# Log-softmax backward on one core: stores moved to a second DMA queue, one group at a time

## Chip, cores, metric

One core of one Trainium2 chip. The metric is device time in microseconds (us) of one execution; each time below is the median of several.

## The reference

```python
def reference(y, dy):                  # both 8 x 1024 x 8192, float32
    softmax_x = np.exp(y)
    sum_dy = np.sum(dy, axis=-1, keepdims=True)
    return dy - softmax_x * sum_dy
```

8192 rows of 8192 elements: 268 MB each of y, dy and output, 805 MB in all, with a few operations per element.

## The kernel before

A group is 256 rows, two per partition, so one partition's share of a tensor is one contiguous run of 64 KiB in HBM. There are 32 groups, two dy tiles `x0` and `x1` (64 KiB per partition each; the result overwrites dy in place) and one y tile of the same size. The parts that matter:

```python
    def sums(x):                       # row 0 on VectorE, row 1 on ScalarE
        ...
        nc.vector.tensor_reduce(out=s_t[:, 0:1], in_=x[:, :D], ..., negate=True)
        for h in range(2):
            nc.scalar.activation(copied[:], x[:, D + h * H : D + (h + 1) * H],
                                 COPY, accum_out=half_t[:, h : h + 1])
        ...
    def compute(x, s_t, r):            # three pieces of a row
        for b, e in PIECES:
            cs = slice(r * D + b, r * D + e)
            nc.scalar.activation(y_t[:, cs], y_t[:, cs], EXP)
            nc.vector.scalar_tensor_tensor(out=x[:, cs], in0=y_t[:, cs], ...)

    for g in range(0, G, 2):           # every DMA on SyncE's queue
        load_dy(g, x_ts[0])
        load_y(g, 0, W)
        s_t = sums(x_ts[0])
        for r in range(R):
            compute(x_ts[0], s_t, r)
        load_dy(g + 1, x_ts[1])
        s_t = sums(x_ts[1])
        for r in range(R):
            load_y(g + 1, r * D, (r + 1) * D)
            compute(x_ts[1], s_t, r)
        for j in range(2):             # a batch of two stores
            nc.sync.dma_start(out=out_v[g + j], in_=x_ts[j][:])
```

So four loads of 8.4 MB (the last in two halves) are followed by two stores of 8.4 MB, all in one queue.

## Time and profile before

| | |
|---|---|
| time, median of 3 | 1867.44 us (1866.99 to 1867.85) |
| moved | 805.3 MB, 432 GB/s over the span |
| busy | DMA 99.9%, VectorE 46%, ScalarE 37% |

The page's rate in 40 equal slices of the span (bytes counted where a packet starts, so single slices jitter by a few per cent):

```profile
GB/s 427 424 430 427 430 447 427 427 431 445 427 427 441 426 437 434 438 431 427 437 438 429 433 428 440 434 431 437 425 438 436 433 436 425 439 433 436 434 428 391
```

**A measure used throughout.** A packet is one contiguous run that one of the 16 DMA engines moves. The trace records each packet's start, duration, size and queue. In an undisturbed stretch a 64 KiB packet takes 2.418 us and one of 32 KiB 1.213 us (in the whole trace before, where all 32 KiB packets are y loads, their median is 1.214). Everything above that, summed over all packets and divided by 16, I call *packet excess*; the time, averaged over the engines, in which an engine had no packet between the first and the last packet is *idle*. With the undisturbed time of all packets the three add up to the span to within 1 us where packets have 32 and 64 KiB: neighbouring packets of one engine overlap by 3 to 4 ns in the records, and this makes up for the 3 us before the first and after the last packet.

### The profile page before, as it was taken

The numbers are of one execution on the slowest core, as the hardware profiler recorded it, in microseconds if no ns is written. First come the engines' busy times: TensorE is split into PE (matmuls) and PEld (weight loads), VectorE is DVE, ScalarE is ACT, GpSimd is POOL, SyncE is SP. The second block draws the span as 40 slices with busy tenths as digits, with TensorE's granted clock in tenths as the row PEclk, the third lists the DMA queues.
The fourth block names the chain that finished last, engine by engine and source line by source line (L and its number), as shares of the span: only waits on it lengthen the run. The fifth ranks groups of instructions, "written<-read, shape, count | busy, mean of one in ns | idle before, by whom it ended". The sixth has DMA issues, their size and how long they took to land.

```text
span 1865.9 us, 923 instructions
## 1 busy us (share of the span) xinstructions
DVE 859.8 (46%) x256; ACT 698.7 (37%) x321; POOL 0.2 (0%) x4
## 2 busy tenths in 40 slices
DVE  2907429074290732807328073280632806338063
ACT  2606326063260532605336052360523605236052
POOL 0000000000000000000000000000000000000000
DMA  9999999999999999999999999999999999999999
GB/s 427 424 430 427 430 447 427 427 431 445 427 427 441 426 437 434 438 431 427 437 438 429 433 428 440 434 431 437 425 438 436 433 436 425 439 433 436 434 428 391
DMA packets 16135, 805.37 MB, mean 432 GB/s; under 512 B 1792, under 2 KB 1792, under 8 KB 1792
## 3 DMA queue, kind: packets, MB, share of 16 engines
q1 hardware_dynamic: 16128, 805.31, 99.9%
q14 instruction: 7, 0.06, 0.0%
HBM read 536.87 MB, written 268.44 MB: 432 GB/s over the span
## 4 chain that ended last, share of the span: by engine, by line
DMA 64%; DVE 13%; ACT 10%; another core or an unknown queue 9%; issue 1%; SPq 0%; DVEq 0%; ACTq 0%
DMA x<-in_dy_dram 31%; DMA out_dram<-x 30%; DVE x L81 13%; ACT copied L61 6%; ACT y_t L80 4%; DMA y_t<-in_y_dram 3%; SPq L75 0%; DVEq L128 0%; ACTq L128 0%; SPq L52 0%; ACTq L80 0%; ACTq L61 0%
## 5 line engine op out<-in xcount | busy, mean ns | idle before, releaser
L81 DVE SCALAR_TENSOR_TENSOR x<-y_t,s_t,x 128x3072 f32<-128x3072 f32 (+1 forms) x192 | 579.4, 3059 | 255.7 <-ACT y_t L80 255.7
L57 DVE TENSOR_REDUCE s_t<-x 128x1 f32<-128x8192 f32 x32 | 277.8, 8682 | 722.3 <-DMA x<-in_dy_dram 722.3
L80 ACT ACTIVATE y_t<-y_t 128x3072 f32<-128x3072 f32 (+1 forms) x192 | 460.1, 2466 | 269.4 <-DMA y_t<-in_y_dram 253.2
L61 ACT ACTIVATE copied<-x 128x4096 f32<-128x4096 f32 x64 | 229.6, 3587 | 864.9 <-DMA x<-in_dy_dram 863.9
L61 ACT ACTIVATION_READ_ACCUMULATOR copied<-x 128x1 f32 x64 | 11.9, 186 | 0.0
L64 DVE TENSOR_SCALAR s_t<-half_t 128x1 f32<-128x1 f32 x32 | 6.5, 204 | 0.0
L61 ACT ACT_TABLE_LOAD x1 | 1.3, 1283 | 0.7 <-PEq L117 0.7
L117 POOL MEMSET const-bfloat16-1.0<- 128x1 bf16 x1 | 0.1, 101 | 0.0
L117 POOL MEMSET const-uint8-127<- 128x1 uint8 x1 | 0.1, 101 | 0.0
L117 POOL MEMSET const-float32-0.0<- 128x1 f32 x1 | 0.1, 98 | 0.2 <-issue 0.2
L117 POOL MEMSET const-float32-1.0<- 128x1 f32 x1 | 0.1, 98 | 0.0
## 6 DMA issues: line engine op xcount, KB each, us to landing
y_t<-in_y_dram SPq DMA_DIRECT2D x32, 4096.0 KB, 18.1
x<-in_dy_dram SPq DMA_DIRECT2D x32, 48.3
out_dram<-x SPq DMA_DIRECT2D x32, 32.5
y_t<-in_y_dram SPq DMA_DIRECT2D x16, 57.6
```

The costliest lines, as they stand in the source:

```text
L57: nc.vector.tensor_reduce(out=s_t[:, 0:1], in_=x[:, :D], axis=mybir.AxisListType.X, op=ALU.add, negate=True)
L61: nc.scalar.activation(copied[:], x[:, D + h * H : D + (h + 1) * H], COPY, accum_out=half_t[:, h : h + 1])
L64: nc.vector.tensor_scalar(out=s_t[:, 1:2], in0=half_t[:, 0:1], scalar1=half_t[:, 1:2], scalar2=-1.0, op0=ALU.add, op1=ALU.mult,)
L80: nc.scalar.activation(y_t[:, cs], y_t[:, cs], EXP)
L81: nc.vector.scalar_tensor_tensor(out=x[:, cs], in0=y_t[:, cs], scalar=s_t[:, r : r + 1], in1=x[:, cs], op0=ALU.mult, op1=ALU.add,)
L117: nc = _bacc.Bacc("TRN2", target_bir_lowering=False, num_devices=1)
```

## The change

Its intent: let each group's store go as soon as the group is ready, on a queue of its own, so that loads never stand behind stores; load y by halves; drop the batches of two. The sum of the second row becomes one ScalarE instruction. The core of the diff (the first part replaces the two 4096-wide copies into PSUM by one of 8192 in place, and makes `load_y` take a row number):

```diff
...
-        for h in range(2):
-            nc.scalar.activation(
-                copied[:], x[:, D + h * H : D + (h + 1) * H], COPY, accum_out=half_t[:, h : h + 1]
-            )
+        nc.scalar.activation(x[:, D:], x[:, D:], COPY, accum_out=second_t[:])
...
-    for g in range(0, G, 2):
-        load_dy(g, x_ts[0])
-        load_y(g, 0, W)
-        s_t = sums(x_ts[0])
+    for g in range(G):
+        x = x_ts[g % 2]
+        load_dy(g, x)
+        s_t = sums(x)
         for r in range(R):
-            compute(x_ts[0], s_t, r)
-        load_dy(g + 1, x_ts[1])
-        s_t = sums(x_ts[1])
-        for r in range(R):
-            load_y(g + 1, r * D, (r + 1) * D)
-            compute(x_ts[1], s_t, r)
-        for j in range(2):
-            nc.sync.dma_start(out=out_v[g + j], in_=x_ts[j][:])
+            load_y(g, r)
+            compute(x, s_t, r)
+            if g == G - 1:
+                if r == 0:
+                    nc.sync.dma_start(out=out_v[g - 1], in_=x_ts[(g - 1) % 2][:])
+                nc.sync.dma_start(out=out_v[g][:, r * D : (r + 1) * D], in_=x[:, r * D : (r + 1) * D])
+        if g < G - 2:
+            nc.scalar.dma_start(out=out_v[g], in_=x[:])
 
 
 # ---- launch: one core; inputs and outputs as the reference has them ----
```

More of the change, by code (lines that the diff above doesn't have):

```diff
@@ L35 @@
     assert N == G * P * R and D == 8192 and G % 2 == 0
-    H = D // 2
     PIECES = [(0, 2048), (2048, 5120), (5120, D)]
@@ L45 @@
     stats = ctx.enter_context(tc.tile_pool(name="stats", bufs=3))
-    psum = ctx.enter_context(tc.tile_pool(name="psum", bufs=1, space=bass.MemoryType.PSUM))
     x_ts = [pool.tile([P, W], fp32, name=f"x{j}") for j in range(2)]
     y_t = pool.tile([P, W], fp32, name="y_t")
-    copied = psum.tile([P, H], fp32, name="copied")
     def load_dy(g, x):
@@ L55, in sums @@
         s_t = stats.tile([P, R], fp32, name="s_t")
-        half_t = stats.tile([P, 2], fp32, name="half_t")
+        second_t = stats.tile([P, 1], fp32, name="second_t")
         nc.vector.tensor_reduce(
@@ L59, in sums, with load_y @@
         )
-        for h in range(2):
-            nc.scalar.activation(
-                copied[:], x[:, D + h * H : D + (h + 1) * H], COPY, accum_out=half_t[:, h : h + 1]
-            )
+        nc.scalar.activation(x[:, D:], x[:, D:], COPY, accum_out=second_t[:])
         nc.vector.tensor_scalar(
-            out=s_t[:, 1:2],
-            in0=half_t[:, 0:1],
-            scalar1=half_t[:, 1:2],
-            scalar2=-1.0,
-            op0=ALU.add,
-            op1=ALU.mult,
-        )
-        return s_t
-    def load_y(g, lo, hi):
-        nc.sync.dma_start(out=y_t[:, lo:hi], in_=y_v[g][:, lo:hi])
+            out=s_t[:, 1:2], in0=second_t[:], scalar1=-1.0, scalar2=None, op0=ALU.mult
+        )
+        return s_t
+    def load_y(g, r):
+        nc.sync.dma_start(out=y_t[:, r * D : (r + 1) * D], in_=y_v[g][:, r * D : (r + 1) * D])
     def compute(x, s_t, r):
```

## The prediction

> **What bounds the kernel now.** I read the page first, for which resource is full; then the DMA windows, for whether reads and writes go at different rates; then the SyncE queue's waits; then the timeline of the last 60 us.
>
> From the page:
>
> ```profile
> span 1865.9 us, 923 instructions
> DVE 859.8 (46%) x256; ACT 698.7 (37%) x321; POOL 0.2 (0%) x4
> DMA  9999999999999999999999999999999999999999
> q1 hardware_dynamic: 16128, 805.31, 99.9%
> HBM read 536.87 MB, written 268.44 MB: 432 GB/s over the span
> ```
>
> VectorE and ScalarE are busy less than half of the time; the DMA engines are at 90% or more in all 40 slices, and the packets of the one hardware queue fill 99.9% of 16 engines' span. The kernel is a copy with arithmetic hidden in it: 805.3 MB that the change does not reduce.
>
> From the windows, one inside a phase of stores and one inside a phase of loads (columns: window, length, busy time of the engines, clock, DMA share, GB/s):
>
> ```profile
> 84.00:118.00 34.00, 8.80 (x3) 4.97 (x2) 0.00 (x0) 1.00 1.00 432
> 124.00:176.00 52.00, 23.38 (x7) 21.74 (x10) 0.00 (x0) 1.00 1.02 444
> ```
>
> Bytes are counted where a packet starts, so short windows jitter by a few per cent. The packet records beneath them are sharper: a packet is one contiguous run in one partition; the 10,240 packets of 64 KiB have a median of 2.418 us and the 4,096 of 32 KiB one of 1.213 us, for loads and stores alike. 65,536 B in 2.418 us is 27.1 GB/s, times 16 engines 433.7 GB/s. Both directions run at the engines' own rate.
>
> From the waits of SyncE's queue:
>
> ```profile
> SPq L75 <- DMA y_t<-in_y_dram: 614.4, 16, 40.0
> SPq L102 <- DVE x L81: 466.3, 16, 29.9
> SPq L52 <- DMA out_dram<-x: 385.1, 30, 18.8
> ```
>
> The queue waits a lot, but the engines have work queued during each of these waits, so none reaches the end of the kernel. Because everything is in one queue in program order, loads and stores hardly ever mix: about 78 us of loads, then 39 us of stores, 16 times.
>
> From the timeline, the end:
>
> ```profile
> 1826.53 7.22 ACT L80 ACTIVATE y_t<-y_t 128x2048 f32<-128x2048 f32 x3 [2.49 <-DMA y_t<-in_y_dram]
> 1834.46 3.41 DVE L81 SCALAR_TENSOR_TENSOR x<-y_t,s_t,x 128x3072 f32<-128x3072 f32 x1
> 1837.90 0.34 SPq L102 DMA_DIRECT2D out_dram<-x  x1
> ```
>
> The last half of y lands at 1826.5 and its arithmetic ends at 1837.9, 11.4 us later. Meanwhile the last-but-one store, 8.4 MB, keeps the DMA engines busy, and the final store follows without a hole. This tail is hidden now.
>
> **What the Trainium skill says.** "DMA: Bandwidth & Descriptors", section "Where 436 GB/s comes from", gives 16 ports of 32 bytes at 850 MHz, 435.2 GB/s. The trace agrees: 432 over the span, 433.7 inside a packet. So 805.3 MB need at least 1850 us, and no order of transfers can gain 2%. The same page, "Issuing engines are not separate DMA queues", says that queues of several issuing engines share the same 16 DMA engines and interleave, and that a second issuer saves only issue time; the kernel before has one queue, so its trace cannot show it. Its section "Queues, rings and completion order" adds that an engine alternates between queues by packet; I use that below to say who finishes when. "ScalarE: Activation LUTs", section "What ACT_TABLE_LOAD costs", gives 186 ns + 0.833 ns per element for an ACTIVATE with immediate operands: 3.60 us for 4096 elements, and the trace has 3.587.
>
> **The change part by part.**
>
> *Sum on ScalarE.* 64 copies of 128x4096 into PSUM (3.587 us each, plus 0.186 to read the accumulator) become 32 in place of 128x8192. By the skill's line these take 7.01 us, so 32 x (2 x 3.77 - 7.20) = 11 us less ScalarE time in the whole kernel. All of it is beside a full DMA: worth 0.
>
> *y in halves.* 16 loads of 8.4 MB become 32 of 4.2 MB; counted per engine, y goes from 128 + 256 packets (64 and 32 KiB) to 512 of 32 KiB. One 64 KiB packet is 2.418, two of 32 KiB are 2.426: 128 x 0.008 = +1.0 us. The final store in halves adds a few hundredths.
>
> *Stores at once, on ScalarE's queue.* Does the DMA keep work? I follow one steady group in packets of one engine (8 per transfer). Take time 0 as store g issuing, right after the last arithmetic on group g. In SyncE's ring there are then the last 3 of 8 packets of dy(g+1), 8 of y's first half, and y's second half becomes issuable at this moment (its buffer is free). Alternating: 3 x (2.42 + 2.42) = 14.5 us; then the store's other 5 packets against 5 of y: 5 x (2.42 + 1.21) = 18.2. Store g lands at about 33 us, and only then may dy(g+2) start, into the same buffer. But SyncE's ring still holds 3 + 8 packets of y, 13.3 us, while a new issue needs 0.4 us and the first packet comes some 1.0 us after the issue (0.73 to 1.75 us at the start of this trace). So no hole. y's second half lands at 46 us, its arithmetic takes the 11.4 us from above, and during it 5 packets of dy(g+2) run: 12 us. Store g+1 then issues at 58 us, with 3 packets of dy left: the cycle closes, at 25.17 MB / 0.4325 = 58.2 us per group, which is the DMA's time. Sums (8.7 us VectorE) fall before y needs them. ScalarE now waits in its own instruction stream for VectorE before each store, about 3 us per group with at least 20 us idle: 0.
>
> *The tail.* "Last two stores behind all loads" is not what the instruction order shows. SyncE's final sequence is: dy(31), y(31) first half, store 30, first half of store 31 (which waits for the arithmetic on that half), y(31) second half, second half of store 31. So the last 4.2 MB load is the last thing in the ring, behind 12.6 MB of stores. When it lands, nothing is left to move until its arithmetic is done: some 0.7 us to landing and release, 11.4 of arithmetic, 0.3 issue, 1.0 to the first packet: a hole of 13.4 us, where the kernel before has none.
>
> Sum without any price of mixing: 1867.4 + 1.0 + 13.4 - 0.5 (a few fixed pauses at the 15 phase changes that go) = 1881 us.
>
> **The rivals.**
>
> 1. *Mixing costs.* After the change each engine switches between a load and a store packet about 8 times in each of 30 groups, 240 turns, where the kernel before has 16 in each direction. For: in its packet records the last y packets before each change to stores are longer than 1.213 us, by 0.006 to 0.2 us per engine, median 0.11 (the very first change 1.0); that is the only place where packets are regularly slow. If each turn cost this, 240 x 0.11 = 26 us, 1907 us. Also, someone wrote batches of two on one queue into a tuned kernel, presumably for a reason. Against: store-to-load changes show no excess; and late in the kernel, where the engines have drifted apart by about 2.5 us and some load while others store, the packets keep 2.418 us. I give a price of some size 40%, and 12 to 15 us as its mean.
>
> 2. *A starved DMA.* Stores share the ring time with loads, so store g lands after 33 us instead of 19, and dy(g+2) waits for it. If round-robin favoured loads more than I assume, the ring could run dry. Against: 13 us of slack above. A hole of 2 us per group would make 1940. I give this 8%.
>
> 3. *More overlap.* Two queues could hide the 8 ns that each packet now pays over its 2.409 us at the skill's rate, and the pauses. At best 1850 + 16.5 = 1867: the same as before. "Perfetto Trace Analysis", section "DMA Optimizations", recommends separate issuers for input and output where it allows more spread; here the spread has nothing to fill. 12%.
>
> 4. *The tail is hidden after all*, if the hardware starts the last load earlier than the queue's order. Against: the order of waits in one queue is fixed. 5%; 1868.
>
> **Range and chances.** 1881 us is the plain sum; 40% of a mixing price of 12 to 15 us gives 1886. Low end: rivals 3 or 4, 1868. High end: a full mixing price and some hole, 1925. Slower by over 2% begins at 1904.8, which needs at least 24 us beyond the tail's 13.4; I give that 0.22. Faster by over 2% is excluded by the 1850 us floor.
>
> **What would show it.** Right: DMA slices of 9 to the last but one, a last slice with a clear dip; a timeline that ends with a y load landing, 11.4 us of arithmetic and then a 4.2 MB store alone; packets of 64 KiB still at 2.42 us; the store's time to landing near 33 us; ScalarE's queue waiting on VectorE. Mixing right: packets of 64 KiB longer while both queues are active, GB/s in all middle slices below 425. Starving right: 8s in the DMA line and compute waiting longer for dy. Wrong altogether: a time under 1870, with no hole before the last store, or over 1925.

## More of the kernel before

For the kernel before: 1858.0 + 4.6 + 2.9 = 1865.5 us, against a span of 1865.9. The three terms are worked out from the packet records; the profile's page does not print them.

## The result, and the profile after

| | before | after |
|---|---|---|
| time, median (range), 4 runs each | 1867.64 us (1866.99 to 1868.19) | 1931.18 us (1923.86 to 1938.28) |
| ratio | 1 | 1.034 (95%: 1.030 to 1.038) |
| packets undisturbed + excess + idle | 1858.0 + 4.6 + 2.9 | 1859.1 + 52.5 + 17.7 |

The change costs 63.5 us, 3.4%. In terms of the ledger: +1.1 from shorter packets, **+47.9 from packets that take longer**, +14.8 from engines with nothing to do.

The page after:

```profile
span 1929.3 us, 933 instructions
...
DVE 862.2 (45%) x256; ACT 691.1 (36%) x257; POOL 0.2 (0%) x4
...
DMA  9999999999999999999999999999999999999996
GB/s 413 424 435 435 446 435 432 422 435 427 403 424 421 418 426 430 427 406 414 421 425 409 408 421 419 421 423 405 420 418 418 420 402 421 427 419 415 422 425 271
...
q1 hardware_dynamic: 14256, 553.65, 67.6%
q10 hardware_dynamic: 4320, 251.66, 31.5%
...
HBM read 536.87 MB, written 268.44 MB: 417 GB/s over the span
```

HBM now moves 417 GB/s over the span in place of 432. Two things are to be seen. The last slice is down to 6 and 271 GB/s: a hole at the end. And the rate sags: the first ten slices are as before, and from the eleventh on most are between 403 and 427, while the DMA line still reads 9. The engines are busy all the time and move less. "Busy" does not tell the two apart; only the rate does.

The stretches make the sag plainer (columns: window, length, busy time of VectorE, ScalarE and GpSimd, clock, DMA share, GB/s). The kernel before:

```profile
500.00:800.00 300.00, 152.41 (x46) 123.36 (x56) 0.00 (x0) 1.00 1.00 432
...
1400.00:1700.00 300.00, 142.35 (x41) 116.34 (x54) 0.00 (x0) 1.00 1.00 432
```

The changed kernel:

```profile
100.00:280.00 180.00, 86.05 (x27) 69.42 (x27) 0.00 (x0) 1.00 1.01 437
500.00:800.00 300.00, 134.71 (x40) 107.78 (x40) 0.00 (x0) 1.00 1.00 423
...
1400.00:1700.00 300.00, 134.71 (x40) 107.78 (x40) 0.00 (x0) 1.00 1.00 417
```

In its first 280 us the changed kernel runs at full rate although its two queues already alternate; the sag comes later. It comes from some of the packets: from 500 to 1700 us the median 64 KiB packet still takes 2.418 us, but 27% of those on ScalarE's queue take over 0.1 us more, and their mean is 2.564 us.

The timeline shows the same in the distance between stores. These are four of the 30 issues on ScalarE's queue (start, length, engine, line, operation), two early neighbours and two late ones:

```profile
112.46 0.36 ACTq L93 DMA_DIRECT2D out_dram<-x  x1
...
170.51 0.36 ACTq L93 DMA_DIRECT2D out_dram<-x  x1
...
1728.56 0.36 ACTq L93 DMA_DIRECT2D out_dram<-x  x1
...
1788.65 0.36 ACTq L93 DMA_DIRECT2D out_dram<-x  x1
```

Early, a group takes 58.05 us, the 58.2 of the prediction's cycle; late, 60.09 us. The next dy load waits until the store from its tile has landed; from the waits of SyncE's queue (total, times, longest) and the page's list of DMA issues (the last number is the median time from issue to landing):

```profile
SPq L51 <- DMA out_dram<-x: 1121.7, 30, 39.3
...
out_dram<-x ACTq DMA_DIRECT2D x30, 38.9
```

The end, from the timeline:

```profile
1879.15 0.55 SPq L66 DMA_DIRECT2D y_t<-in_y_dram  x1
...
1906.04 7.22 ACT L71 ACTIVATE y_t<-y_t 128x2048 f32<-128x2048 f32 x3 [31.47 <-DMA y_t<-in_y_dram]
...
1910.63 6.75 DVE L72 SCALAR_TENSOR_TENSOR x<-y_t,s_t,x 128x3072 f32<-128x3072 f32 x2 [0.30 <-ACT y_t L71]
1917.41 0.33 SPq L91 DMA_DIRECT2D out_dram<-x  x1
```

The last half of y lands at 1906.0, its store issues at 1917.4, and in between there is nothing to move. Where the timeline of before had a store of 8.4 MB beside this arithmetic, there is now none.

### The profile page after: what moved, and what is told of

Read it like the earlier page. It is cut to its first block, busy times and chain, and to the rows that moved or that the text cites. A ratio compares the mean times of both kernels' runs of the same rounds, so it can differ in the third digit from the quotient of the medians.

```text
span 1929.3 us, 933 instructions
## 1 busy us (share of the span) xinstructions
DVE 862.2 (45%) x256; ACT 691.1 (36%) x257; POOL 0.2 (0%) x4
## 4 chain that ended last, share of the span: by engine, by line
DMA 80%; DVE 11%; ACT 8%; issue 0%; DVEq 0%; ACTq 0%; SPq 0%
DMA y_t<-in_y_dram 80%; DVE x L72 11%; ACT y_t L71 8%; DVEq L119 0%; ACTq L119 0%; ACTq L71 0%; SPq L51 0%; SPq L91 0%; SPq L66 0%
## 5 line engine op out<-in xcount | busy, mean ns | idle before, releaser
L59 ACT ACTIVATE x<-x 128x8192 f32<-128x8192 f32 x32 | 225.0, 7030 | 557.8 <-DMA x<-in_dy_dram 557.8
L59 ACT ACTIVATION_READ_ACCUMULATOR x<-x 128x1 f32 x32 | 6.0, 187 | 0.0
L60 DVE TENSOR_SCALAR s_t<-second_t 128x1 f32<-128x1 f32 x32 | 4.6, 144 | 0.0
```

Source lines behind the costliest of these rows:

```text
L59: nc.scalar.activation(x[:, D:], x[:, D:], COPY, accum_out=second_t[:])
L60: nc.vector.tensor_scalar(out=s_t[:, 1:2], in0=second_t[:], scalar1=-1.0, scalar2=None, op0=ALU.mult)
```

## The experiments

The question: what stretches the packets. Theory A: packets get longer while some of the 16 engines load from HBM and others store to it. Rival B: a second queue as such costs. Rival C: giving up the batches of two costs, because the one stream changes direction more often. More theories come up on the way. Runs with a wrong result are named; they are there for their traces.

### One queue again, without batches (one_queue)

```diff
     for g in range(G):
         load_dy(g, x)
         s_t = sums(x)
...
+        if g > 0:
+            nc.sync.dma_start(out=out_v[g - 1], in_=x_ts[(g - 1) % 2][:])
         for r in range(R):
             load_y(g, r)
             compute(x, s_t, r)
...
-        if g < G - 2:
-            nc.scalar.dma_start(out=out_v[g], in_=x[:])
```

and at the end, both halves of the last y before the last stores.

> The changed kernel with its stores moved back to SyncE's queue, each group's store behind the next group's dy load, no batches of two, and the tail as in tail_loads_first. Theory A (packets stretch while some of the 16 engines load from HBM and others store to it): loads and stores no longer run at once, so packets go back to 2.418 us and the time to 1867 to 1872. Theory B (a second queue as such costs): the same, 1867 to 1872. Theory C (giving up the batches of two costs, by twice as many changes of direction in the queue): most of the loss stays, 1900 or more.

Measured: 1868.89 us (ratio 1.0009, 0.9992 to 1.0026), excess 4.7, idle 3.1. Its rate in the same stretches:

```profile
500.00:800.00 300.00, 141.18 (x43) 114.99 (x43) 0.00 (x0) 1.00 1.00 434
...
1400.00:1700.00 300.00, 143.42 (x42) 114.90 (x42) 0.00 (x0) 1.00 1.00 433
```

This undoes the whole loss. Rival C falls: 31 changes from loads to stores in place of 16, no batches, and the time of before. The single ACTIVATE for the sum and y in halves are in this kernel too, so they cost nothing to speak of.

### The tail alone (tail_loads_first)

```diff
+        if g == G - 1:                 # both y halves first, then compute, then the stores
+            for r in range(R): load_y(g, r)
+            for r in range(R): compute(x, s_t, r)
+            ... the three last stores on SyncE's queue
```

> The changed kernel with one edit at the end: both halves of the last y are issued before the last stores, so that something is left to move while the last arithmetic runs. If the hole at the end (about 13 us between the last y packet and the first packet of the last store) is real time, the kernel gets 13 us faster: 1931 to about 1918, with the sum of packet excess (packet time over 2.418 or 1.213 us, summed over 16 engines and divided by 16) unchanged near 45 to 50 us. If the hole only shifts other waiting, the time stays at 1931.

Measured: 1926.59 us, 4.6 less than the 1931.18 of the changed kernel, where 13 were expected: in the time a miss. In the profiled runs the idle time at the end fell from 15.7 to 4.9 us, as expected. But this run had some 8 us more idle time spread over its middle, engines that had got ahead and ran dry while others were still at an earlier transfer. The hole is real; with a spread of 14 us between the changed kernel's own runs, four runs don't show its full worth in the time. The run "reload" below shows it better.

### Only reading, with the same waits (reload; wrong result)

```diff
         if g < G - 2:
-            nc.scalar.dma_start(out=out_v[g], in_=x[:])
+            nc.scalar.dma_start(out=x[:], in_=y_v[G - 1 - g])
```

> Wrong result on purpose. The changed kernel with each of the 30 stores on ScalarE's queue replaced by a load of the same size into the same tile (8.4 MB of y), with the same waits before and after it: two queues alternate as in the changed kernel, but both read. Theory A (the direction: stores to HBM while other engines load): the packet excess falls from about 48 to under 10 us, and the time to 1880 to 1888, what the hole at the end leaves. Theory E (not the direction but two interleaved streams that keep meeting each other in a bad alignment, as phase_toggle suggests, which became free of loss by shifting): excess stays at 30 us or more, 1915 or more.

Measured: 1881.16 us (ratio 1.0077), excess 4.8, idle 15.1. Its rate in the same stretches:

```profile
500.00:800.00 300.00, 143.51 (x43) 114.59 (x44) 0.00 (x0) 1.00 1.01 435
...
1400.00:1700.00 300.00, 138.86 (x41) 111.91 (x41) 0.00 (x0) 1.00 1.00 433
```

Same two queues, same alternation, same waits, same sizes; only the direction of 30 transfers differs, and with it their place in HBM (y instead of the output), and the stretched packets are gone. That settles two things. Rival B falls: two queues by themselves cost nothing that shows (excess 4.8 us, against 4.6 before). And what is left, 1881.2 us, is the hole at the end plus the shorter packets, the very sum of the prediction without mixing.

### The control, and other addresses (after_again, out_reversed)

The first is the changed kernel once more. The second stores to the output's groups in reverse order (wrong result):

```diff
-            nc.scalar.dma_start(out=out_v[g], in_=x[:])
+            nc.scalar.dma_start(out=out_v[G - 3 - g], in_=x[:])
```

> The changed kernel unchanged, as the control for the two others of this call and a second trace of it. Time 1924 to 1938 as its four runs; packet excess 40 to 55 us; the hole before the last store about 13 us again.

> Wrong result on purpose. The changed kernel with the 30 stores on ScalarE's queue going to the output's groups from the end to the start, waits and sizes unchanged. If the loss depends on which HBM addresses a load and a store have at the same time, the excess moves by a third or more against after_again; if it is only a matter of both directions at once, it stays within 10 us of it and the time is 1920 to 1940.

Measured: 1932.21 us with excess 43.8 and idle 27.4; and 1935.98 us with excess 51.8 and idle 25.1. Both are as expected. Reversing the stores changes nothing beyond the spread (43.8 and 52.5 for the unchanged kernel in two traces). Which group a store goes to makes no difference larger than that. Finer address relations were not tried here. The control also shows how far two traces of one kernel differ: its excess begins at about 200 us and not at 280, 33.5 us of its 43.8 are in packets of SyncE's queue (24.7 of 52.5 in the first trace), and it has 27.4 us of idle time in place of 17.7.

### Loads and stores without arithmetic (mix_free; wrong result)

```python
    for k in range(2 * n):             # 128 loads of 4.2 MB, four buffers
        nc.sync.dma_start(out=ld[k % 4][:], in_=(dy_v if k < n else y_v)[k % n])
    for k in range(n):                 # 64 stores, independent of the loads
        nc.scalar.dma_start(out=out_v[k], in_=src[:])
```

> Wrong result on purpose. No arithmetic: 128 loads of 4.2 MB on SyncE's queue and, independent of them, 64 stores of 4.2 MB from one zeroed tile on ScalarE's queue; all packets are 32 KiB. Stores end after some 1250 us and then loads run alone. Theory A: packets stay at 1.213 us while the engines are in step, and stretch (mean 1.26 to 1.32 us) in the mixed part once they have drifted; at 1.213 again in the part with loads alone. Total 1900 to 1950. If the loss needs the real kernel's waits and arithmetic, 1862 to 1870.

Measured, in one run: 1867.99 us, excess 3.5. Each engine alternates load, store, load, store, packet by packet for 1250 us, and every packet keeps 1.213 us. So theory A as first stated, "directions mixed on two queues are slow", is not enough. In this trace all 16 engines stay in step within 0.55 us: 55% of the time they all load or all store. But that is also a mixture: in 41% of the time (the packet records sampled every 50 ns) 3 to 13 engines store while the others load, and nothing is lost. In the changed kernel's trace such a mixture fills 11% of the time from 120 to 280 us, the fast stretch, and 40% from 500 to 1700 us, with stores under way in somewhat over half of it. So the engines do fall out of step there, but the share of mixed time alone does not set the price.

### The same without writing HBM (mix_no_hbm_write; wrong result)

```diff
-        nc.scalar.dma_start(out=out_v[k], in_=src[:])
+        nc.scalar.dma_start(out=dst[k % 2][:], in_=src[:])
```

> Wrong result on purpose. As mix_free, but the transfers on ScalarE's queue go from one SBUF tile to another, so that two queues are mixed and drift is possible but HBM is only read (the two last copies excepted). If the loss comes from HBM being read and written at once, packets stay at 1.213 us and the total is 1862 to 1875. If it comes from the second queue, the engines or the SBUF side, packets stretch as in mix_free and the total is 1900 or more.

Measured, in one run: 2122.32 us, a miss of both expectations and not a clean test. The copies from SBUF to SBUF are slow beside the loads: their packets took 1.62 us in the mean instead of 1.213, which makes 367 GB/s for copies and loads together until the copies end:

```profile
GB/s 373 368 367 371 364 368 366 368 369 367 367 370 365 368 368 368 367 368 367 367 367 367 368 368 365 373 375 389 394 425 432 432 431 433 431 431 432 432 431 316
```

One thing can be read from it: nearly all loads from HBM kept 1.213 to 1.215 us (median and mean beside the copies, after the first 20 us), although the engines were far out of step. In the changed kernel packets of the load queue are stretched as well (24.7 of the 52.5 us of excess). This points to the writes to HBM, and does not prove it.

### Putting engines out of step on purpose (phase_toggle, phase_toggle_64k, phase_toggle_reversed; wrong result)

```diff
     for k in range(2 * n):
+        if k in (8, 24, 40, 56):       # 8 partitions x 1 KiB
+            nc.sync.dma_start(out=tiny[:], in_=dy_v[0][0:8, 0:256])
         nc.sync.dma_start(out=ld[k % 4][:], in_=...)
```

The second uses 64 KiB packets (tiny loads at 4, 12, 20, 28), the third stores from the end of the output to its start.

> Wrong result on purpose. As mix_free (128 loads of 4.2 MB on SyncE's queue, 64 independent stores on ScalarE's, packets of 32 KiB), with four tiny loads of 8 partitions x 1 KiB put into SyncE's queue before loads 8, 24, 40 and 56. A transfer of 8 partitions runs on 8 of the 16 engines; on those it takes one turn of the alternation, so that they store while the other 8 load, until the next tiny load turns it back. In step from 0 to about 155 us, out of step to 465, in step to 775, out of step to 1085, in step to 1240, then loads alone. Theory A (a packet stretches when other engines move data the other way at the same time, and being in step hides it): packets at 1.213 us in the in-step stretches, longer by 5 to 15% out of step; total 1890 to 1930. Theory D (phase does not matter; the real kernel loses by something else, such as addresses or its waits): 1.213 us everywhere, total 1868 to 1872.

> Wrong result on purpose. As phase_toggle with 64 KiB packets both ways (64 loads and 32 stores of 8.4 MB, tiny loads before loads 4, 12, 20 and 28), the size of the real kernel's dy loads and stores. Theory A: 2.418 us in step, 5 to 15% longer out of step, total 1890 to 1930. If only long packets are hurt[...], this run loses and phase_toggle does not. Theory D: 1868 to 1872.

> Wrong result on purpose. As phase_toggle, with the stores going through the output from its end to its start, so that loads and stores meet at other addresses. If the loss out of step comes from loads and stores that fall on the same places of HBM, it changes by half or more against phase_toggle; if from the direction alone, the stretch out of step is the same within a fifth.

Measured, in one run each: 1890.03, 1871.72 and 1874.57 us, with an excess of 13.3, 9.7 and 7.1 us. The rate of phase_toggle in three stretches, after the first tiny load and later:

```profile
100.00:280.00 180.00, 0.00 (x0) 0.00 (x0) 1.00 1.00 417
500.00:800.00 300.00, 0.00 (x0) 0.00 (x0) 1.00 1.00 433
...
1100.00:1400.00 300.00, 0.00 (x0) 0.00 (x0) 1.00 1.00 429
```

After the first tiny load (eight packets of 1 KiB at 148 us), about half of the engines do store while the others load, and store packets then take 0.1 to 0.5 us longer, but only on some engines, and only until about 300 us. From there to 1080 us the excess is at most 0.06 us per 100 us although 3 to 13 engines are storing in 67% of the time, also where the plan had them in step. After the last tiny load, at 1085 us, comes a second burst of 2.8 us, until the stores end; it is in the third line above. The excess falls unevenly, the engines end between 1864.5 and 1886.8 us, and so 13.3 us of it make a time at the edge of theory A's range; the stretches do not go as A said. In phase_toggle_64k all of the excess is in loads, and it is at most 0.02 us per 100 us between 900 and 1200 us with such a mixture in 97% of the time. So opposite directions at the same moment can be slow and can be free. In a stream that runs on undisturbed, the stretched packets shift the engines against each other until nothing is lost any more; the kernel with its bursts of eight packets per engine does not get there, or is thrown out of it by each new burst. That last sentence is my reading, not a thing that a run took apart. The reversed addresses nearly halved the excess (13.3 to 7.1 us), one run each; half was to point at addresses, so addresses stay open.

### Bringing the engines into step (in_step)

```diff
             load_y(g, r)
+            if r == 1 and 0 < g < G - 1:   # the next dy load must wait for this
+                nc.sync.dma_start(out=x_ts[(g + 1) % 2][0:1, 0:1], in_=y_t[0:1, W - 1 : W])
             compute(x, s_t, r)
```

> The changed kernel, still two queues with loads and stores alternating, but each next dy load (g from 2 on) is made to wait until the current group's second y half has landed (a 4-byte copy from the y tile into the tile that dy will overwrite). So in each of 30 groups all 16 engines run empty for about 2 to 3 us and start the next load together: 60 to 90 us of added idle time, on purpose. If the stretched packets come from engines that have drifted out of step (some storing while others load), the packet excess falls from 44 to 52 us to under 15 and idle rises by 60 to 90: total 1960 to 1990. If alternating loads and stores on two queues costs whether in step or not, the excess stays above 35 us and the total is 1990 to 2025.

Measured: 2131.31 us, excess 110, idle 157: a clear miss. In 20 of the 30 groups the order of loads stayed as meant. There the engines start together, and the trace shows what that costs: the first load packet takes 0.4 to 0.9 us longer on most engines, the last load before the first store 0.9 to 1.6 us longer, and then load and store alternate eight times at the undisturbed times (read from one such group, 978 to 1020 us in the packet records). In the other 10 groups the scheduler put a y load ahead of dy; there (a group at 1036 to 1085 us) 64 KiB loads and stores alternate with the engines a microsecond and more apart, and both are stretched, loads by up to 2.0 us and stores by up to 0.7, packet after packet. So alternation in step is free, entering it is not, and forcing the step is no remedy. The engines' step explains part of the loss and not all of it.

### Changing direction often on one queue (one_queue_turns, one_queue_cut, one_queue_halves)

The store of one_queue cut into quarters that take turns with quarters of y; the same quarters one after the other, not in turn; and halves in turn.

```diff
-            nc.sync.dma_start(out=out_v[g - 1], in_=x_ts[(g - 1) % 2][:])
-        for r in range(R):
-            load_y(g, r)
+            for c in range(0, W, 4096):          # turns; 8192 for halves
+                piece = slice(c, c + 4096)
+                nc.sync.dma_start(out=out_v[g - 1][:, piece], in_=x_ts[(g - 1) % 2][:, piece])
+                nc.sync.dma_start(out=y_t[:, piece], in_=y_v[g][:, piece])   # cut: in a second loop
```

> one_queue with each store and the y loads behind it cut into four pieces of 2.1 MB (16 KiB runs) that follow one another in turn, store, load, store, load, on the one queue: 8 changes of direction per group in place of 2, and 12,288 shorter packets. Smaller packets alone: about 3 us. If the price is a turn's (0.11 us per engine and load-to-store change, as the prediction priced it), 31 x 3 more such changes add 10 us: 1882. If the price comes with two queues whose engines choose their next packet for themselves, nothing more is added: 1870 to 1875. If fine mixing of directions costs by itself, 1890 or more.

> one_queue with the store cut into four consecutive pieces of 16 KiB runs and the y loads likewise, not in turn: two changes of direction per group as in one_queue, packet lengths as in one_queue_turns. one_queue_turns lost 46 us of packet excess, 30 us of it in the last 64 KiB dy packet ahead of the first store piece (0.93 us each, 0.08 in one_queue), nothing inside the fine alternation. If the short runs behind a long one are the trigger, that 0.9 us per change stays and the time is about 1910 to 1920. If the alternation of directions is the trigger, the excess falls under 12 us and the time is 1878 to 1888 (12 us of it from shorter packets).

> one_queue with the store in two halves of 32 KiB runs, each followed by one half of y: four changes of direction per group, packets no shorter than the changed kernel's y. If alternation is the trigger: excess between one_queue's 5 and one_queue_turns' 46, about 15 to 40, time 1882 to 1908. If only 16 KiB runs bring it: excess under 8, time 1870 to 1875.

| | time | packets undisturbed | excess | idle |
|---|---|---|---|---|
| one_queue (whole) | 1868.89 | 1859.1 | 4.7 | 3.1 |
| one_queue_halves | 1869.69 | 1861.1 | 3.5 | 4.0 |
| one_queue_cut | 1877.53 | 1869.7 | 4.2 | 5.4 |
| one_queue_turns | 1920.21 | 1869.7 | 46.1 | 5.4 |

One queue is no protection by itself: with quarters in turn it loses as much as the changed kernel. Neither are short packets the trigger (one_queue_cut pays only their fixed cost, 8.6 us of time more than one_queue, or 10.6 summed over packet records that overlap) nor alternation as such (one_queue_halves is free). In one_queue_turns the loss is not in the alternation either: 29.7 of the 46.1 us are in the last dy packet ahead of the first store piece, 0.93 us each, where one_queue has 0.08; and 6.6 us in the first dy packet after the last piece. So the price of one change from loads to stores runs from nothing to a microsecond, by circumstances that these runs do not single out. **This stays open.**

## Why the prediction was wrong

The measured 1931 us lies above the range (1868 to 1925); to slower by over 2%, which it is, I gave 0.22.

**Right.**
- The bound: the DMA engines, before and after. (The floor of 1850 us is an estimate from the skill's 435.2 GB/s; at the 433.7 GB/s measured inside a packet it is 1857.) VectorE and ScalarE are as idle as before, and the lighter sum brought nothing, as said (each of its instructions takes 7.03 us, 7.01 expected; ScalarE's busy time went from 698.7 to 691.1 us, where 11 us less were expected).
- The cycle, in the early part: 58.2 us per group expected, 58.05 measured. The alternation packet by packet on which it rests is what mix_free shows. Store g+1 issues 11.4 us after y's second half begins its arithmetic (101.08 to 112.46), as taken from the trace before. In the early part the next dy, which waits for the store, issued 34.5 us after it (112.46 to 146.92), against 33 expected.
- The tail: the last load stands behind the stores in SyncE's queue, and the hole is there: 13.4 us expected, and about 13 us more idle time at the end than before in the changed kernel. "reload" has the tail without the mixing and takes 1881.2 us; the prediction's sum without mixing was 1881.

**Half right: no starved DMA.** In the profiled run rival 2 did not happen: up to 60 us before its end the engines were idle for 1.8 us in all. In the control and in out_reversed it is 8.8 us, in tail_loads_first 10.5. There engines that have emptied their queues stand still, for up to 4 us, and nearly always the next thing they get is a dy load that has waited for a store to land. Late in the run a store holds the next dy load back for 39 us (1728.56 to 1767.71) and not for 33, and the 13 us of slack are no longer enough for every engine.

**Wrong: one term, the price of mixing.** Rival 1 is what happened, and its sign is in the profile, though not as cleanly as I had put it: part of the 64 KiB packets are longer while both queues are active, and from the eleventh slice on most, not all, are under 425 GB/s. But its size failed twice. I took 0.11 us per change from loads to stores, times 240, 26 us at most; the measured excess is 47.9 us above the kernel before, which is 0.2 us for each of the 240. And I gave it 40% and let 5 us into the number, because I read two "against" lines from the trace before as evidence that mixing is free: that store-to-load changes show no excess, and that engines 2.5 us apart keep 2.418 us. Both were true of a kernel in which a mixture lasts at most 2.5 us at each of two changes in every 116 us. They said nothing of one in which it lasts 33 us in every 58.

**Wrong: the model under the number.** A price per turn does not describe it. While the engines keep in step, the turns are free (mix_free, though 41% of its time is mixed; the first 280 us of the changed kernel; the alternations of in_step's regular groups, once entered). Out of step they cost up to 2 us a packet, or, in a long undisturbed stream, nothing again. What separates the free mixtures from the dear ones these runs do not show. The early stretch where a kernel still runs in step is just what one would look at to check a small price, and it would have misled.

**Ledger of the difference.** 1886 predicted, 1931 measured, 45 us: some 43 from the price of mixing (47.9 in place of 5), the rest within the spread of the runs. The sizes are those of one trace: in the control some 65 us of loss are 39.2 of longer packets and 24.5 of idle time.

**What is shown and what is not.** Shown: beside the hole at the end, the loss is for the most part in stretched packets; these go when whole stores stay in one queue with the loads, and when the second queue reads; a second queue by itself, the lost batches, the sum, y in halves, the order of output groups and short packets by themselves are not the cause. Not shown: which resource makes a load wait when other engines store. The direction matters (in reload together with the place in HBM), and so, it seems, does how the engines stand to each other in time; no run separates HBM from the path to it, and finer relations of addresses stay open.

## What to carry to other kernels

When the DMA engines are already full in one well-ordered queue, a second queue for the stores has nothing to gain and can lose 2.6% (47.9 us here, beside the hole at the end): keep long stretches of loads and whole stores in one queue, and batches are then not needed either (one_queue without them: 1868.9 us). Read the rate beside the busy share: a slice at 417 GB/s and one at 432 GB/s both show a 9 in the DMA line. And see what is last in the queue: a load that only stores stand ahead of exposes its arithmetic at the end, 13 us here, whatever the description of the change says about its order.

## What the Trainium skill lacked or had wrong

- "DMA: Bandwidth & Descriptors", "Issuing engines are not separate DMA queues": says that queues interleave and that a second issuer only saves issue time. It lacks that loads on one queue and stores on another can lower the total rate: 416 to 423 GB/s here from 500 to 1700 us, in place of 432 to 434 before and 431 to 435 when both queues read. The suggestion of "Perfetto Trace Analysis", "DMA Optimizations", to give input and output separate issuers should carry this warning; the change did so and lost 3.4%, 47.9 of its 63.5 us by longer packets.
- No page tells what a change of direction on a DMA engine costs. The runs show 0.08 us (one_queue) to 0.93 us (one_queue_turns) per engine in the last packet before a change from loads to stores, and nothing for many changes.
- "DMA: Bandwidth & Descriptors", "Why small descriptors are slow", gives about 3 cycles of fixed cost per packet. At 32 bytes per cycle of 850 MHz, 64, 32 and 16 KiB would take 2.409, 1.205 and 0.602 us; the records have 2.418, 1.213 and 0.611, 8 to 9 ns more. But neighbouring records overlap by 3 to 4 ns; from start to start packets take 2.414, 1.210 and 0.607, so that 5 ns are left, some 4 cycles by this estimate, little more than the page has. (The 8 ns of the prediction's rival 3 are about 5 for the same reason.)
- "SBUF — State Buffer", in its rules, says to use about 358 GB/s for HBM to SBUF and 436 only for SBUF to SBUF, without a word on how many cores run. With one core running the runs show 432 to 434 for HBM both ways, and 367 for loads from HBM and copies from SBUF to SBUF together; copies from SBUF to SBUF alone were not run.
